# A transformer pair on one core: 96 bytes ahead of the weight tiles, the last strip's banks, the order of the constant tables, and one copy on another engine

## The chip, the cores and the metric

The kernel runs on one core of a Trainium2 chip. The metric is the device time of one execution in microseconds (us). Of the kernel before there are three timed executions, and one more that was profiled. Engines: TensorE (PE, with its weight loads PEld), VectorE (DVE), ScalarE (ACT), GpSimd (POOL), and SyncE (SP), which here only issues DMAs.

## The reference, cut to what matters

Two transformer blocks run one after the other over x, 256 tokens of 1024 channels in fp32. Each linear layer below is a product of the (normed) tokens with a weight matrix; together with the tables they make nearly all of the 191.47 MB read.

```python
# first block
h = rmsnorm(x, norm_mix)
fq, fk, fv, ff, gq, gk, gv, gb, ga, gz, sq, sk, sv, gates = split(h @ w_in)
ya = fox_attention(...); yb = gated_delta_rule(conv(gq, gk, gv), ...); yc = stick_breaking_attention(...)
x = x + (g0 * (ya @ w_oa) + g1 * (yb @ w_ob) + g2 * (yc @ w_oc)) @ w_out
x = x + memory_cross_attention(rmsnorm(x), rmsnorm(mem), w_mq, w_mkv, ..., w_mo)
x = x + conv_ffn(rmsnorm(x), w_up, ffn_conv, ffn_conv_b, w_down)
# second block
x = x + 0.5 * rmsnorm(swiglu(rmsnorm(x), ...), ffn1_post_g)
x = x + rmsnorm(concat(moba_attention(...), multiscale_pool(...)) @ w_out, mix_post_g)
x = x + rmsnorm(memory_cross_attention_2(...), xa_post_g)
x = x + 0.5 * rmsnorm(swiglu(rmsnorm(x), w_gate, w_up, w_down), ffn2_post_g)
```

`rmsnorm(x, g)` is x / sqrt(mean(x*x) + 1e-6) * g over the 1024 channels.

## The kernel before, in words

**Layout and pieces.** The tokens lie channel by channel (128 partitions, 8 groups, 256 tokens) in `x`. Every weight matrix is streamed from HBM once, in pieces of at most 128 x 1024 fp32 (512 KB). A piece lands in `raw` (three buffers, `load_weight`, issued on SP), is then split by `split_weight` into a high part `wh` (ACT copies it, rounded to the type fp32r that PE multiplies) and a low part `wl` (DVE, `raw` less `wh`), four buffers each. Activations are split in the same way into `hi` and `lo` tiles of the pool `a`. PE forms three products for each piece, hi·wh, lo·wh and hi·wl, and adds them up in banks of PSUM.

**Jobs and banks.** A job is a strip of output columns of one layer, with one to several pieces. Kind "a" has the weights stationary and 256 tokens moving (matmuls 128x256), kind "b" has the activation stationary and 512 weight columns moving (128x512). A job takes its banks from the pool `pmm` (three banks, `PMM`) when its first piece starts, in `products`, and gives them back when its callback has evicted them. All the small work beside it (attention, the delta rule, norms), called chains, works in the pool `pat` (five banks, `LIMIT`), which `room`, `take` and `drop` share out. The names in the profile follow: `pmm<-a,wh` is a product of a weight piece, `pat<-...` a chain's matmul, and `raw`, `wh`, `wl` are the piece's tiles.

**Who sets the order.** All instructions are put out in one order by a planner that runs while the program is built. `Pace` (`issue`) models each engine's time with costs written in the code; `Stream.pick` takes the next piece from a window of split pieces, by `start_of`, which returns None for a job that hasn't begun as long as the `pmm` banks in use and its own would be more than three. Between pieces, `step` advances the chains (generators that are due) and calls `split`, which splits a piece and asks for the loads up to three pieces on. On the chip each engine then works through its own queue in that order, with semaphores between engines; the DMAs of one queue are issued in the order in which SP meets them. The order of the first strips is `FIRST_ORDER`.

**The start (from line 2013).** SP issues `x` in four parts with the first weight pieces between them, then `vec` (line 2025: gains and convolution taps, all but the few columns that an earlier DMA on ACT's queue, `vec0`, brought). A chain `constants` asks for the first half of `con` once 5 pieces have been loaded, for its second half at 9 and for `poolw` at 40. `start` splits the activations, `start_sq` squares x and adds up the squares, and `sq_rows` turns the sum into a row `rb` of 1/sqrt for all tokens: it adds the two halves (`one`), splits the sum into `hi` (a copy on ACT) and `lo` (a subtraction on the engine it is given, DVE for the first norm, GpSimd for the others), sums over partitions with a matmul with ones into a `pat` bank, and takes Ln and Exp on ACT. The first jobs' evictions multiply by `rb`, so they can't run before it.

**The end.** `result` (line 1536) is the last layer, 2816 to 1024 channels, with two jobs of kind "b", one for each half of the output channels; each job has two banks, one for each 128 tokens. The second job is made with `last=True`; its `held` list keeps the last two pieces back, and `last_pieces` runs them first for the one bank and then for the other. The first job's callback `cb` squares and multiplies both banks on ACT and DVE.

**Pools.** The pools are allocated in SBUF in the order x, c, a, s2, s1, tiny, sq, rb, wh, wl, raw (`build`, line 2042).

## Time and profile before

| | |
|---|---|
| median of 3 runs | 1154.55 us (1153.91 to 1156.99) |
| profiled execution | 1154.29 us, span 1152.5 us, mean granted clock of PE 0.994 |
| PE | 98% of the span busy, 9108 matmuls |
| DVE, ACT, POOL | 66%, 58%, 22% |
| DMA | 193.96 MB in all, 168 GB/s over the span |

The span runs from the first to the last recorded instruction. A row of a timeline gives start, length, engine, line, operation, output<-inputs, size and count, and in brackets how long the engine had been idle and what released it; the line is nearly always L291, that of the helper through which the planner issues. [...]

### The profile page before, as it was taken

What the parts mean: (1) busy time and instruction counts of PE and PEld (TensorE: products, weight loads), DVE (VectorE), ACT (ScalarE), POOL (GpSimd) and SP (SyncE); (2) the same over time, 40 slices, a digit from 0 to 9 for tenths busy, and PEclk for the clock granted to TensorE, in tenths of its full rate; (3) what the DMA queues carried; (4) which work ended last, traced back from release to release, by engine and by line L of the source; (5) the groups of instructions that cost most, each with busy time, mean ns of one, the idle gap of its engine ahead of it and who ended that gap; (6) DMA issues with size and microseconds to landing.
All of it is one profiled execution on the core that took longest, in us unless ns stands there. A gap on an engine that the chain in (4) does not pass through costs nothing.

```text
span 1152.5 us, 22341 instructions
## 1 busy us (share of the span) xinstructions
PE 1126.1 (98%) x9108; PEld 1074.6 (93%) x9108; DVE 762.5 (66%) x1015; ACT 668.1 (58%) x1085; POOL 250.1 (22%) x235
## 2 busy tenths in 40 slices
PE   8999999999999999999999999999999998999997
PEld 7998998999988999999999999999989998999976
DVE  6885785558886588998556555448876747555543
ACT  5447773465786566666545554546667557555442
POOL 0020130022141023333015333012102112533200
PEclk9999999999999999999999999999999999999999
DMA  7554533236564365556656555665444534666652
GB/s 244 180 170 152 193 111 111 93 111 199 169 200 146 101 193 183 183 183 190 203 160 218 191 190 177 201 194 160 167 148 147 152 92 140 205 192 207 196 191 91
DMA packets 56550, 193.96 MB, mean 168 GB/s; under 512 B 6400, under 2 KB 6528, under 8 KB 56448
## 3 DMA queue, kind: packets, MB, share of 16 engines
q1 hardware_dynamic: 56304, 192.54, 52.3%
q8 instruction: 71, 1.16, 0.4%
q14 instruction: 31, 0.25, 0.1%
q10 hardware_dynamic: 144, 0.01, 0.0%
HBM read 191.47 MB, written 1.05 MB: 167 GB/s over the span
## 4 chain that ended last, share of the span: by engine, by line
PE 65%; DVE 16%; ACT 7%; issue 6%; DMA 4%; POOL 1%; SPq 0%; DVEq 0%; ACTq 0%; POOLq 0%
PE pmm L291 58%; PE pat L291 8%; DVE wl L291 6%; ACT wh L291 3%; DVE s L291 3%; DVE a L291 3%; DMA raw<-w_in 3%; ACT s L291 2%; DVE g L291 1%; DMA raw<-w_up 1%; DVE sg L291 1%; DVE ypad L291 1%; POOL s L291 1%; ACT g L291 1%; ACT L291 1%
## 5 line engine op out<-in xcount | busy, mean ns | idle before, releaser
L291 DVE TENSOR_TENSOR wl<-raw,wh 128x1024 fp32r<-128x1024 f32 (+1 forms) x370 | 455.3, 1238 | 283.1 <-ACT wh L291 279.4
L291 PE MATMUL pmm<-a,wh 128*128 128x256 f32 x3856 | 505.0, 281 | 7.2 <-DVE a L291 5.2
L291 PEld LDWEIGHTS pmm<-a,wh 128*128 128x128 f32 x3856 | 474.3, 189 | 13.3 <-DVE a L291 6.9
L291 ACT ACTIVATE wh<-raw 128x1024 fp32r<-128x1024 f32 (+1 forms) x370 | 372.5, 1019 | 166.4 <-PE pmm L291 58.1
L291 PE MATMUL pmm<-a,wl 128*128 128x256 f32 x1928 | 269.8, 281 | 2.4 <-DVE wl L291 1.8
L291 PEld LDWEIGHTS pmm<-a,wl 128*128 128x128 f32 x1928 | 244.0, 188 | 5.8 <-DVE wl L291 4.4
L291 PE MATMUL pmm<-g,wh 128*128 128x256 f32 x1088 | 140.3, 280 | 0.1
L291 PEld LDWEIGHTS pmm<-g,wh 128*128 128x128 f32 x1088 | 132.6, 188 | 0.8 <-POOL g L291 0.3
L291 POOL TENSOR_TENSOR sq<-sq,sq 128x512 f32<-128x512 f32 x30 | 41.9, 1398 | 342.4 <-ACT sq L291 304.9
L291 POOL TENSOR_TENSOR s<-s 128x256 f32<-128x256 f32 x66 | 71.9, 1089 | 175.7 <-ACT s L291 169.3
L291 ACT ACTIVATE s<-s 128x256 f32<-128x256 f32 (+4 forms) x118 | 56.1, 478 | 91.2 <-DVE s L291 76.9
L291 POOL TENSOR_TENSOR g<-s,g 128x256 fp32r<-128x256 f32 x66 | 64.5, 978 | 60.0 <-ACT g L291 60.0
L291 PE MATMUL pmm<-g,wl 128*128 128x256 f32 x544 | 75.6, 280 | 0.0
L291 PEld LDWEIGHTS pmm<-g,wl 128*128 128x128 f32 x544 | 68.7, 188 | 0.1
L291 ACT ACTIVATE g<-s 128x256 fp32r<-128x256 f32 x66 | 27.3, 413 | 56.7 <-POOL s L291 56.7
L291 PE MATMUL pmm<-wh,g 128*128 128x512 f32 x208 | 55.4, 405 | 2.9 <-DVE a L291 1.9
L291 POOL TENSOR_TENSOR s<-s,s 128x512 fp32r<-128x512 f32 (+1 forms) x25 | 33.4, 1342 | 105.7 <-ACT s L291 101.0
L291 PEld LDWEIGHTS pmm<-wh,g 128*128 128x128 f32 x208 | 39.8, 193 | 13.0 <-DVE a L291 2.2
L291 DVE SCALAR_TENSOR_TENSOR s<-ypad,vec,s 128x256 f32<-128x256 f32 x88 | 45.7, 578 | 0.0
L291 PE MATMUL pmm<-wh,a 128*128 128x512 f32 x160 | 42.0, 401 | 0.0
L291 DVE TENSOR_TENSOR s<-pmm,rb 128x512 f32<-128x512 f32 x44 | 30.2, 688 | 16.1 <-PE pmm L291 16.1
L291 ACT ACTIVATE a<-x,vec 128x256 fp32r<-128x256 f32 x54 | 24.8, 501 | 21.5 <-DVE x L291 21.4
(165 smaller groups left out, 874.5 us busy)
## 6 DMA issues: line engine op xcount, KB each, us to landing
raw<-ffn_w_up SPq DMA_DIRECT2D x82, 512.0 KB, 4.2
raw<-w_in SPq DMA_DIRECT2D x78, 512.0 KB, 4.3
raw<-ffn_w_down SPq DMA_DIRECT2D x42, 512.0 KB, 4.3
raw<-w_up SPq DMA_DIRECT2D x41, 512.0 KB, 4.3
raw<-w_down SPq DMA_DIRECT2D x20, 512.0 KB, 4.3
raw<-w_out SPq DMA_DIRECT2D x16, 512.0 KB, 4.4
raw<-xa_wkv SPq DMA_DIRECT2D x16, 512.0 KB, 4.0
raw<-w_mkv SPq DMA_DIRECT2D x8, 512.0 KB, 4.1
```

Source lines behind the costliest of these rows:

```text
L291: return fn(*args, **kwargs)
```

## The change: four edits

1. A pool `gap` with one tile of 24 fp32 (96 bytes in each partition) is allocated between `rb` and `wh`, so that `wh`, `wl` and `raw` lie 96 bytes higher.
2. The last job (the one with a `held` list) takes its two banks from `pat`. In `start_of`, such a job no longer counts as a user of `pmm`; it may start when two `pat` banks are free in the model.
3. The DMA of `vec` moves from right behind the x loads into the chain `constants`, where it is asked for once 6 pieces have been loaded; the first half of `con` moves from 5 to 9, the second from 9 to 26. `poolw` stays at 40.
4. In `sq_rows`, the copy to `hi` runs on DVE when the engine given is DVE, which is so for the first norm alone.

```diff
+GAP = 24
...
         if job not in self.begun:
-            live = sum(len(j.ps) for j in self.begun + self.pending)
-            if live + job.banks > PMM - (pc is not self.window[0]):
+            live = sum(len(j.ps) for j in self.begun + self.pending if j.held is None)
+            if job.held is not None:
+                if len(self.K.live["pat"]) < job.banks or sorted(self.K.live["pat"])[job.banks - 1] > self.pace.now + SLACK:
+                    return None
+            elif live + job.banks > PMM - (pc is not self.window[0]):
                 return None
...
         if job.ps is None:
-            job.ps = [K.pmm() for _ in range(job.banks)]
+            if job.held is None:
+                job.ps = [K.pmm() for _ in range(job.banks)]
+            else:
+                job.ps = [K.pat().rearrange("p (a b) -> p a b", a=2) for _ in range(job.banks)]
             self.begun.append(job)
...
         hi, lo = (parts2[:, i, :] for i in range(2))
-        nc.scalar.activation(hi, one, AF.Copy)
+        if eng is nc.vector:
+            nc.vector.tensor_copy(hi, one)
+        else:
+            nc.scalar.activation(hi, one, AF.Copy)
         self.tt(lo, one, hi.bitcast(F32), ALU.subtract, eng)
...
-    nc.sync.dma_start(K.vec, aps["vec"][:, NVEC0:])
 
     def constants():
         half = CON["negtri"][0]
-        for n, dst, src in ((5, K.con[:, 0:half], aps["con"][:, 0:half]), (9, K.con[:, half:], aps["con"][:, half:]),
-                            (40, K.poolw, aps["pool_w"])):
+        for n, dst, src in ((6, K.vec, aps["vec"][:, NVEC0:]), (9, K.con[:, 0:half], aps["con"][:, 0:half]),
+                            (26, K.con[:, half:], aps["con"][:, half:]), (40, K.poolw, aps["pool_w"])):
...
-        pools = {n: (pool(n, b, **({"space": PSUM} if n in ("pmm", "pat") else {})), b) for n, b in bufs.items()}
+        pools = {}
+        for n, b in bufs.items():
+            if n == "wh":
+                pools["gap"] = (pool("gap", 1), 1)
+            pools[n] = (pool(n, b, **({"space": PSUM} if n in ("pmm", "pat") else {})), b)
         K = Kern(tc, pools, aps)
+        K.p["gap"].tile([P, GAP], F32, name="gap")
```

## Rows read from the trace of the kernel before

**Rows 1.** The page, busy time of each engine.

```profile
PE 1126.1 (98%) x9108; PEld 1074.6 (93%) x9108; DVE 762.5 (66%) x1015; ACT 668.1 (58%) x1085; POOL 250.1 (22%) x235
```

**Rows 2.** Windows, `pmm` matmuls alone: window, its length, PE busy (count), clock, DMA share, GB/s.

```profile
0.00:1153.00 1153.00, 1032.02 (x7968) 0.99 0.53 168
```

**Rows 3.** Timeline of PE: three stretches of the same products.

```profile
1010.55 2.03 PE L291 MATMUL pmm<-a,wh 128*128 128x256 f32 x16
1012.42 1.09 PE L291 MATMUL pmm<-a,wl 128*128 128x256 f32 x8
...
300.98 2.04 PE L291 MATMUL pmm<-g,wh 128*128 128x256 f32 x16
302.87 1.10 PE L291 MATMUL pmm<-g,wl 128*128 128x256 f32 x8
...
598.98 2.08 PE L291 MATMUL pmm<-a,wh 128*128 128x256 f32 x16
600.90 1.12 PE L291 MATMUL pmm<-a,wl 128*128 128x256 f32 x8
```

**Rows 4.** Timeline of PE and of DVE near the start.

```profile
26.25 0.50 PE L291 MATMUL pat<-onesr,s 128*128 128x1 f32 x4
29.50 0.88 PE L291 MATMUL pmm<-a,wh 128*128 128x256 f32 x4 [2.75 <-DVE a L291]
...
25.55 0.42 DVE L291 TENSOR_TENSOR s<-s,s 128x256 fp32r<-128x256 f32 x1
...
27.55 1.23 DVE L291 TENSOR_TENSOR wl<-raw,wh 128x1024 fp32r<-128x1024 f32 x1 [0.23 <-ACT wh L291]
```

**Rows 5.** Timeline of PE near the end.

```profile
1114.16 0.39 PE L291 MATMUL pmm<-wh,g 128*128 128x512 f32 x1
1115.59 0.97 PE L291 MATMUL pmm<-wh,g 128*128 128x512 f32 x3 [1.04 <-DVE sg L291]
```

**Rows 6.** Timeline of SP's DMA issues near the start.

```profile
15.98 0.43 SPq L291 DMA_DIRECT2D con<-con  x1
...
22.19 0.33 SPq L291 DMA_DIRECT2D raw<-w_in  x1
```

**Rows 7.** Chain that ended last, near the start: start, length, what.

```profile
17.53 5.68 DMA raw<-w_in
```

**Rows 8.** DMA issues: count, KB each, median us from issue to landing.

```profile
raw<-w_in SPq DMA_DIRECT2D x78, 512.0 KB, 4.3
...
con<-con SPq DMA_DIRECT2D x1, 800.0 KB, 5.5
con<-con SPq DMA_DIRECT2D x1, 404.0 KB, 4.6
vec<-vec SPq DMA_DIRECT2D x1, 172.5 KB, 5.0
```

**Rows 9.** Timeline of ACT near the start.

```profile
23.32 1.06 ACT L291 ACTIVATE wh<-raw 128x1024 fp32r<-128x1024 f32 x1 [2.67 <-DMA raw<-w_in]
24.28 0.40 ACT L291 ACTIVATE s<-s 128x256 fp32r<-128x256 f32 x1
...
26.46 1.06 ACT L291 ACTIVATE wh<-raw 128x1024 fp32r<-128x1024 f32 x1 [0.40 <-PE pat L291]
27.43 0.46 ACT L291 ACTIVATE rb<-pat,vec 128x258 f32<-128x258 f32 x1
```

**Rows 10.** Windows: window, its length, busy PE, PEld, DVE, ACT, POOL, clock, DMA.

```profile
29.92:33.34 3.42, 3.42 (x18) 3.42 (x17) 3.35 (x9) 3.02 (x6) 0.00 (x0) 0.50 0.97 378
33.34:36.75 3.41, 3.41 (x31) 3.41 (x30) 3.34 (x7) 1.43 (x2) 0.00 (x0) 1.00 0.03 8
```

**Rows 11.** Timeline of ACT and DVE: the first readers of `vec` and `con`.

```profile
30.07 1.31 ACT L291 ACTIVATE g<-ypad,vec 128x256 f32<-128x256 f32 x3 [1.74 <-DVE ypad L291]
...
48.78 0.69 DVE L291 TENSOR_TENSOR_SCAN row<-con,row 68x256 f32<-68x256 f32 x1
...
122.80 0.42 DVE L291 TENSOR_TENSOR s<-s,con 128x256 f32<-128x256 f32 x1
```

## The prediction

> **What bounds the kernel now.** I read the page first, for the engine that has no room left, then TensorE's rows for what its time is made of, and then the places where it waits. TensorE (PE) is busy for 1126.1 of 1152.5 us, 98% [rows 1]. The products of the weight pieces with the activations, all the matmuls whose output is a `pmm` bank, are 7968 instructions, and together they cover 1032.0 us at a mean granted clock of 0.99 [rows 2]. The reader is to see two things in this. Whatever is done on VectorE (DVE), ScalarE (ACT) or a DMA queue counts only where TensorE stands still for it, and the idle sum is only 26.4 us. And a change that touches every one of the 7968 matmuls by one nanosecond is worth 8 us, as much as a third of all the idle time.

> So the cadence comes next. The same instruction, 128x256 in fp32r, is not always equally fast: sixteen of them from 1010.55 to 1012.42 are 1.87/16 = 116.9 ns apart, sixteen from 300.98 to 302.87 are 118.1 ns, sixteen from 598.98 to 600.90 are 120.0 ns, all at full clock [rows 3]. Nearly all of the run stands at the first value, in which case 1032 us is its floor.

> Then the two waits on the path that this change touches. Near the start, PE idles for 2.75 us until 29.50, for `a` from DVE [rows 4]: all three `pmm` banks are full, and their eviction wants the first norm's row `rb`. At the end, the last strip's second 512-column matmul starts 1.43 us after its first (1115.59 less 1114.16) and has waited for DVE's `sg`, an eviction of the job before [rows 5].

> The profiled execution took 1154.29 us with a span of 1152.5, so 1.8 us lie around the span; the median of the three runs is 1154.55. I sum against 1154.29 and add 0.2 at the end for that difference.

> **The change part by part.**

> *The last strip's banks.* The last job takes two banks of `pat`, whose chains are done by then, and no longer waits for the eviction of the strip before. What is left is the ordinary distance of two 512-column matmuls, twice 116.9 = 234 ns: 1.43 − 0.23 = **1.2 us saved**. Everything behind it moves up, since PE runs on from there without an idle gap and the last evictions follow its end. Below this, nothing is saved if something else is late at the same place; the piece is split and its activation is there, as its first matmul has run. The rule that lets the last job start outside the `pmm` count moves nothing else, since the job before it stands ahead in the window. I keep 0 and −1.3 as ends.

> *The constant tables.* On the SP queue, the first half of `con` (404 KB, 4.6 us from issue to landing) stands at 15.98 in front of the piece issued at 17.53, which takes 5.68 us to land where the median of such pieces is 4.3 [rows 6 to 8]. ACT has then been idle for 2.67 us and takes the piece at 23.32 [rows 9]. In its place the change puts `vec` (172.5 KB [rows 8]); `con`'s first half goes where the 800 KB of its second half [rows 8] stood (26 us), and the second half goes out behind piece 26, some 70 us in. The queue ahead of the piece at 17.53 becomes shorter by 404 − 172.5 = 231.5 KB. At 378 GB/s (the rate of the stretch from 29.92 [rows 10]), that is 0.6 us.

> How much of this reaches PE? Follow the norm back from 29.50 [rows 4, 9]. The evictions wait for `rb`, whose first half (Ln) runs on ACT at 27.43, straight behind the split copy `wh` at 26.46; that copy is the one of the piece issued at 22.19 (22.19 + 4.3 = 26.5 [rows 6, 8]), so the norm waits in ACT's queue behind a landing. On DVE the split `wl` at 27.55 stands ahead of the evictions in the same way. The issue at 22.19 does not move, as it waits for an earlier split to free its buffer; what moves is its landing, because the two pieces before it have drained earlier. I take **0.5 us saved**: less than the 0.6 that the queue gives, as a landing in 3.7 us or so is the quickest that I would expect of 512 KB. The floor behind it: the norm's matmuls in PE's own queue end at 26.25 + 0.50 = 26.75, and Ln can't start before that, so at most 27.43 − 26.75 = 0.68 is there to be had. Ends: 0 (the landing stays as it is) and −0.68. What is late next is `rb` itself and the eviction, which stay.

> The later uses: `vec` is first needed by the convolution's taps at 30.07, `con`'s first half by a scan at 48.78, its second half at 122.80 [rows 11]. `vec` issued near 16 lands near 21, the first half issued near 26 near 31, the second half issued near 70 near 76. All are in time by 9 us or more, so no wait is added. The 800 KB put near 70 delay one weight piece by 800/378 = 2.1 us at most, once; the same bytes leave the stretch around 30, where the DMA share is 0.97 [rows 10]. PE has three split pieces in hand (2.8 us each, three times 24 matmuls at 117 ns), so I cost it at **nothing**; without that cover it is +2.1, and if the earlier stretch had been limited by those bytes, −0.5.

> *The norm's high part on DVE.* ACT loses a copy of 0.40 us at 24.28 [rows 9], DVE gets one ahead of the subtraction at 25.55 [rows 4]. That subtraction reads two tiles of this size and takes 0.42 us on DVE; a copy reads one, so I put it at no more than 0.4. Behind it on DVE stand the subtraction, which PE's norm matmuls wait for, and the next splits. The piece ahead of it on DVE comes 0.6 us earlier, by the same shorter queue, and a hop from ACT back to DVE goes, so the subtraction is not later than before. **Nothing**; ends: −0.1 and, if it delays the split at 27.55, +0.4.

> *The gap.* It adds no instruction. The 96 bytes shift the addresses of `wh`, `wl` and `raw`, hence every operand that ACT, DVE, PE and the DMA queues read or write for the weights. What could that change? Nothing in the rows ties a duration to an address: the three values of [rows 3] belong to the same tiles and the same shapes, and I found the same pairs of buffers in all of them. From above the price is bounded by the whole run falling from 116.9 to 118.1 ns, 7968 × 1.2 = +9.6 us, or at 120.0 to +24.7; from below by the slower stretches going away, at a tenth of the matmuls (my estimate of their number) × 1.2 ns = −1.0. I take **0**, because most of the run already has the lower value and a shift of all three tiles by one amount leaves their places relative to each other as they are.

> [...]

> The sum: 1154.29 − 1.2 − 0.5 = 1152.6, and 0.2 for the median: **1152.8 us**, 0.15% faster.

> **The rivals.**

> *A, faster: the shorter wait at the start also keeps the clock up.* [...] If the wait became so short that the clock stayed, 13 × 0.117 = 1.5 us more would go: 1151.3. For it: the wait is the only thing ahead of the fall. Against it: by my sum 2.2 of 2.75 us stay. Chance 0.18.

> *B, slower: the addresses matter for PE after all.* If the shift puts the weight reads into the slower cadence of 118.1 for the whole run, the time is 1152.8 + 9.6 = 1162.4. It decides from the point where the other gains are eaten and 0.3% is passed: (3.5 + 1.7)/0.0012 = 4300 of 7968 matmuls. For it: three cadences exist and something selects them. Against it: nothing in the rows selects them by address. Chance 0.10.

> [...] Chance 0.03.

> *D, it does not do what it says: the bank of the last strip was not all that was late, or the earlier landing is swallowed by ACT's queue.* Then one or both terms are zero, up to 1154.5. Chance 0.08.

> The forecast itself has 0.61.

> **How the numbers follow.** A difference of 0.3% (3.46 us: under 1151.1 or over 1158.0) is about what a measurement here tells from no change. The forecast's own ends are 1152.8 − 0.1 − 0.2 − 0.5 − 0.1 − 1.0 = 1150.9, all lower ends together, and 1152.8 + 1.2 + 0.5 + 2.1 + 0.4 = 1157.0, all covers gone together. The range reaches down to A with the same lower ends, 1151.3 − 1.9 = 1149.4, and up to 1156.6, just inside the upper end; outside lie B, C and little else. Faster by over 0.3%: C, half of A (its value lies beside the limit), and 0.11 for the forecast with the gap's lower end, 0.23. Slower: B and 0.01 for a delay that I haven't seen, 0.11. Between them 0.66.

> **What would show it.** In the profile after: the last strip's second 512-column matmul about 0.23 us behind its first, with no idle time put down to DVE `sg`; `vec` issued near 16 and the following piece landing in under 5.2 us; PE's idle ahead of the first long run near 2.2 us, followed by 18 matmuls at half clock (A: 31); no wait for a DMA longer than before near 70 to 80 us; sixteen 128x256 matmuls at 1.87 us near 1010, and the whole `pmm` group at 1032 less the 1.2 or so. I am wrong if the `pmm` group's busy time moves by more than 3 us with the count the same: then addresses select the cadence. I am wrong in a term if the idle at the end or at the start is as long as before.

## The result, and the profile after

The changed kernel takes 1143.43 us (median of 4 runs, 1141.36 to 1145.09) against 1155.28 us before; the ratio is 0.9896, with a 95% interval of 0.9871 to 0.9920. I had forecast 1152.8 with a range from 1149.4 to 1156.6. The profiled execution took 1144.74 us, 9.55 less than the one of before.

Ahead of everything else, the page's first lines, which answer to [rows 1]:

```profile
span 1142.9 us, 22344 instructions
...
PE 1111.7 (97%) x9108; PEld 1060.7 (93%) x9108; DVE 761.7 (67%) x1016; ACT 667.8 (58%) x1084; POOL 251.6 (22%) x235
```

The reader is to take two differences from them. TensorE's busy time fell by 1126.1 − 1111.7 = 14.4 us with the same 9108 matmuls, and its idle time rose by 31.2 − 26.4 = 4.8 us; together these are the 9.6 us by which the span is shorter. So the matmuls themselves became cheaper. The timeline of PE in two stretches shows it (start, length, operation, count), and answers to [rows 3]:

```profile
621.27 1.98 PE L292 MATMUL pmm<-a,wh 128*128 128x256 f32 x16
623.08 1.07 PE L292 MATMUL pmm<-a,wl 128*128 128x256 f32 x8
...
1011.26 2.05 PE L292 MATMUL pmm<-a,wh 128*128 128x256 f32 x16
1013.14 1.11 PE L292 MATMUL pmm<-a,wl 128*128 128x256 f32 x8
```

From 621.27 to 623.08, start to start, there are 16 matmuls in 1.81 us, 113 ns each: a cadence that the kernel before never held for a stretch. (The row's own length, 1.98, reaches past the start of the next row.) From 1011.26 to 1013.14 the same instruction with the same address class takes 117.5. Averaged over long stretches the two are 113.33 and 117.78 ns. Over all 7170 or so distances between neighbouring 128x256 matmuls, the mean went from 116.87 to 114.89 ns (7416 x 1.98 = 14.7 us), and that of the 512-column matmuls from 233.2 to 229.6 (552 x 3.6 = 2.0 us). The two make 2.3 us more than the busy time shows; that difference is not resolved.

In this profile the start became worse, not better. Timelines of PE, of SP's issues and of ACT, then windows (window, length, busy PE, PEld, DVE, ACT, POOL, clock, DMA), which answer to [rows 4, 6, 9, 10]:

```profile
26.37 0.50 PE L292 MATMUL pat<-onesr,s 128*128 128x1 f32 x4
31.04 3.75 PE L292 MATMUL pmm<-a,wh 128*128 128x256 f32 x16 [4.16 <-DVE a L292]
...
16.38 0.42 SPq L292 DMA_DIRECT2D vec<-vec  x1
17.73 4.71 SPq L292 DMA_DIRECT2D raw<-w_in  x3
22.49 0.43 SPq L292 DMA_DIRECT2D con<-con  x1
...
27.91 1.06 ACT L292 ACTIVATE wh<-raw 128x1024 fp32r<-128x1024 f32 x1 [2.19 <-DMA raw<-w_in]
28.87 0.46 ACT L292 ACTIVATE rb<-pat,vec 128x258 f32<-128x258 f32 x1
...
30.19:33.60 3.41, 2.56 (x12) 2.59 (x13) 3.37 (x9) 2.08 (x5) 0.00 (x0) 0.50 0.57 201
33.60:37.02 3.42, 3.42 (x18) 3.42 (x18) 3.42 (x10) 1.64 (x2) 0.00 (x0) 0.50 0.04 14
```

PE idles for 4.16 us where it idled for 2.75, and the half clock behind it (granted 0.50) lasts for 6.8 us where it lasted for 3.4. The piece that the norm waits for was issued at 22.11 and landed at 27.81; `con`'s first half went out at 22.49, right behind it. One profile of each kernel is not enough to lay this on the edit: in a second profile of the changed kernel the idle is 3.08 us, and in one of a kernel with the gap and the banks alone, its tables where they were before, it is 4.08. Timelines of PE, in this order:

```profile
29.84 1.43 PE L292 MATMUL pmm<-a,wh 128*128 128x256 f32 x6 [3.08 <-DVE a L292]
```

```profile
30.14 1.22 PE L292 MATMUL pmm<-a,wh 128*128 128x256 f32 x4 [4.08 <-DVE a L292]
```

The end did what was forecast (timeline of PE, answers to [rows 5]): the last strip is now `pat<-wh,g`, follows without a break, and eight matmuls take 1.84 us, 230 ns each.

```profile
1106.50 2.00 PE L292 MATMUL pat<-wh,g 128*128 128x512 f32 x8
1108.34 1.07 PE L292 MATMUL pat<-wl,g 128*128 128x512 f32 x4
```

Where the other idle time comes from is in PE's waits (who waited for whom: total us, times, longest), the changed kernel's:

```profile
PE pmm L292 <- DVE a L292: 7.6, 7, 4.2
PE pmm L292 <- DVE wl L292: 3.2, 7, 1.1
PE pmm L292 <- ACT wh L292: 3.1, 6, 1.5
PE pat L292 <- POOL s L292: 2.9, 4, 1.4
```

In the kernel before these rows read 7.0, 1.8, 1.7 and 1.6. With cheaper matmuls PE reaches the splits and the chains before these are done: 1.4 + 1.4 + 1.3 us of the gain were given back there; with 1.4 more at the start and 1.0 less at the end this is nearly all of the 4.8. The next two runs bear it out: with the gap alone PE idles for 32.3 us, with the three other edits alone for 27.3.

### The profile page after: what moved, and what is told of

It is laid out like the page before. It is cut to its first block, busy times and chain, and to the rows that moved or that the text cites. A ratio compares the mean times of both kernels' runs of the same rounds, so it can differ in the third digit from the quotient of the medians.

```text
span 1142.9 us, 22344 instructions
## 1 busy us (share of the span) xinstructions
PE 1111.7 (97%) x9108; PEld 1060.7 (93%) x9108; DVE 761.7 (67%) x1016; ACT 667.8 (58%) x1084; POOL 251.6 (22%) x235
## 4 chain that ended last, share of the span: by engine, by line
PE 67%; DVE 14%; ACT 7%; issue 5%; DMA 4%; POOL 1%; DVEq 0%; ACTq 0%; POOLq 0%
PE pmm L292 56%; PE pat L292 11%; DVE wl L292 6%; ACT wh L292 3%; DVE a L292 2%; DVE s L292 2%; DVE g L292 2%; ACT s L292 1%; DMA raw<-w_in 1%; DVE sg L292 1%; ACT L292 1%; DMA raw<-ffn_w_up 1%; DVE ypad L292 1%; ACT g L292 1%; POOL s L292 1%
## 5 line engine op out<-in xcount | busy, mean ns | idle before, releaser
L292 PE MATMUL pmm<-a,wh 128*128 128x256 f32 x3856 | 498.1, 280 | 9.7 <-DVE a L292 5.8
L292 PEld LDWEIGHTS pmm<-a,wh 128*128 128x128 f32 x3856 | 468.1, 189 | 16.0 <-issue 5.1
L292 PE MATMUL pmm<-g,wh 128*128 128x256 f32 x1088 | 137.4, 278 | 0.4 <-DVE g L292 0.4
L292 PEld LDWEIGHTS pmm<-g,wh 128*128 128x128 f32 x1088 | 130.1, 188 | 1.0 <-DVE g L292 0.6
L292 ACT ACTIVATE g<-s 128x256 fp32r<-128x256 f32 x66 | 27.3, 413 | 56.8 <-POOL s L292 56.8
L292 PEld LDWEIGHTS pmm<-wh,a 128*128 128x128 f32 x160 | 29.4, 188 | 6.8 <-DVE g L292 0.7
L292 DVE SCALAR_TENSOR_TENSOR a<-x,vec,a 128x256 fp32r<-128x256 f32 x56 | 32.9, 622 | 2.3 <-ACT a L292 2.3
```

The costliest lines, as they stand in the source:

```text
L292: return fn(*args, **kwargs)
```

## The experiments

The theory after the result (G): the gap alone gives the gain, because the start addresses of weights and activations set the cadence. Rivals: O, the order of the constants or the engine of the copy gives it; and of the addresses, W (the weights' alone), R (weights and moving tile relative to each other), H (not they, but history and traffic).

**Each half of the change by itself.** The kernel before with only the gap, and the changed kernel without it:

```diff
# e1_gap_only: before, and
+GAP = 24
+                pools["gap"] = (pool("gap", 1), 1)
+        K.p["gap"].tile([P, GAP], F32, name="gap")
# e2_no_gap: after, without these three lines
```

> The kernel before with the gap of 96 bytes and no other edit. Theory G (the gap alone gives the gain, through TensorE's cadence): 1144 us (1142 to 1147), the 128x256 cadence 113.3 ns over long stretches as in the changed kernel, idle at the start 2.75 us and the 1.43 us at the end unchanged. Rival O (the order of constants, or the engine of the copy, gives it): 1155 us, cadence 116.9.

> The changed kernel without the gap, the three other edits kept. Theory G: 1154.5 to 1157 us (the 1.2 us of the last strip saved, some 2.5 to 3 us lost at the start, where TensorE's idle is 4.2 us and the half clock lasts 6.8 us), cadence 116.9. Rival O: 1143 to 1145 us.

The gap alone: 1141.27 us (1140.73 to 1145.20), ratio 0.9883 (0.9866 to 0.9900). Without it: 1155.9 us, ratio 1.0000 (0.9986 to 1.0014). G holds and O falls: the three other edits together are worth nothing that can be measured. The lines of busy time from the two pages, the gap alone first, then the change without it:

```profile
PE 1106.6 (97%) x9108; PEld 1054.9 (93%) x9108; DVE 761.8 (67%) x1015; ACT 669.1 (59%) x1085; POOL 251.8 (22%) x235
```

```profile
PE 1125.9 (98%) x9108; PEld 1075.8 (93%) x9108; DVE 763.0 (66%) x1016; ACT 668.5 (58%) x1084; POOL 253.1 (22%) x235
```

Only PE and PEld differ, by 19 and 21 us; DVE and ACT, which read and write the same shifted tiles, stay within 1.2 us.

**TensorE alone, 20 pairs of addresses.** 

```diff
+STA = (0, 4, 8, 16, 24)      # fp32 past a multiple of 128 bytes: weights
+MOV = (0, 8, 16, 24)         # moving tile
+for r in range(2):
+    for s in STA:
+        for m in MOV:
+            stop()           # a small matmul that waits for DVE
+            config(s, m, 8)  # 8 pieces of 24 matmuls 128x256
```

> This kernel computes none of the blocks: TensorE alone multiplies zeros, in the kernel's own pattern (pieces of 24 fp32r matmuls 128x256: hi.wh, hi.wl, lo.wh, a weight load each), with nothing else running. The weights start 0, 16, 32, 64 or 96 bytes past a multiple of 128 bytes, the moving tile 0, 32, 64 or 96 bytes past one, all 20 pairs, each for 192 matmuls, the whole list twice. Theory W (the weights' address alone sets the cadence): about 113.3 ns at one class of the weights' address (0 and 64, or 0 alone), 116.7 at 32 and 96, whatever the moving tile's. Theory R (the address of weights and moving tile relative to each other): the fast pairs form a diagonal of the table. Theory H (addresses are not it, only the history of the run and the other engines' traffic): one cadence for all 20 pairs, or another one in the second pass than in the first.

Mean ns from one matmul to the next at full clock, by the bytes past a multiple of 128 (where the second pass differs by over 0.5 it stands behind a stroke):

| weights \ moving | 0 | 32 | 64 | 96 |
|---|---|---|---|---|
| 0 | 120.0 / 118.7 | 117.8 / 116.7 | **113.3** | 120.0 |
| 16 | 118.3 | 120.0 | 116.7 | 117.8 |
| 32 | 120.0 | 120.0 | 117.3 | 117.8 |
| 64 | **113.3** | 120.0 | 120.0 | 118.7 |
| 96 | 116.7 / 117.8 | 117.8 | 120.0 | 120.0 |

Two rows of its timeline for each of two pairs, weights/moving 0/0 and 64/0; each row is a piece of 24, 2.88 and 2.72 us from start to start:

```profile
15.61 3.04 PE L1363 MATMUL pmmb<-moa,wha 128*128 128x256 f32 x24
18.49 3.04 PE L1363 MATMUL pmmc<-moa,wha 128*128 128x256 f32 x24
...
307.80 2.88 PE L1363 MATMUL pmmc<-moa,whd 128*128 128x256 f32 x24
310.52 2.88 PE L1363 MATMUL pmma<-moa,whd 128*128 128x256 f32 x24
```

Apart from the small writes between the pairs no other engine worked in this time, so H falls as the whole story: addresses count. W falls too, since 0 and 64 are each fast with one moving tile and slow with the other three. R holds in part. The fast pairs are no diagonal, as 32/96 and 96/32, which also lie 64 apart, take 117.8; the two fast ones are those with both tiles on multiples of 64 bytes, in opposite halves of 128. In the kernel, `a` starts at 44608 and `g` at 93760, both 64 past a multiple of 128, and all their buffers are 4096 bytes apart; `wh` starts at 184096 before (32 past: the pair 32/64) and at 184192 after (the pair 0/64). These addresses are those of the compiled programs. Three pairs had two cadences in two passes, so something besides the addresses counts too. And the table is not the kernel: the pair 32/64 takes 117.3 here, but 116.7 or 117.8 over long stretches of the kernel before. Why is not shown; the kernel takes the products in another order.

**The same in the kernel.** A gap of 32 bytes gives the pair 64/64; 64 bytes ahead of `a` and 96 ahead of `wh` give 64/0.

```diff
# g32_same_parity: e1_gap_only with
-GAP = 24
+GAP = 8
# s64_swapped: e1_gap_only with a second gap
+        K.p["gapa"].tile([P, 16], F32, name="gapa")   # ahead of the pool a
```

> The kernel before with a gap of 32 bytes in place of none (the changed kernel has 96) and no other edit: the weights then start 64 bytes past a multiple of 128, as the activations do. Theory R (fast only where weights and moving tile both lie on multiples of 64 bytes and in opposite halves of 128): the pair 64/64 ran at 120.0 ns alone, so the cadence is near 120 and the time 1155.5 + 8520 x 3.1 ns = about 1180 us (1172 to 1184). Theory W (weights on a multiple of 64 bytes are enough, the moving tile does not matter): 113.3 ns and 1141 us, as with 96 bytes.

> The kernel before with 64 bytes ahead of the pool of the activations and 96 ahead of the weights: activations on a multiple of 128 bytes, weights 64 past one, the changed kernel's pair the other way round. No other edit. Theory R: 113.3 ns in long stretches and 1139 to 1145 us, as with the gap alone. Rival (the weights must lie on multiples of 128, or it is the distance to raw or to the edge of the memory that counts): no gain, 1155 us or more.

32 bytes: 1166.97 us, ratio 1.0081 (1.0057 to 1.0106), slower than with no gap at all. The direction is R's and against W; the size that I had put on it (1172 to 1184 us) was some 2.5 times too large. The 128x256 cadence rose by 3.0 ns as expected (119.88 in the mean), but a 512-column matmul fell from 233.2 to 228.0, and part of the rest had been idle time of PE before (26.4 us, here 1165.1 − 1142.2 = 22.9). Swapped: 1151.1 us (1143.38 to 1157.08), ratio 0.9943 (0.9916 to 0.9969): a gain, so not the distance to `raw` or to the memory's edge; but smaller and much more scattered than forecast. The profiled one (1145.33, among the fastest of the eight) has 113.3 over the same stretch in which 32 bytes have 120; what the slower ones, up to 1157.08, held was not profiled. Timelines of PE, 32 bytes first, then swapped:

```profile
1011.21 2.08 PE L292 MATMUL pmm<-a,wh 128*128 128x256 f32 x16
1013.13 1.12 PE L292 MATMUL pmm<-a,wl 128*128 128x256 f32 x8
```

```profile
1010.29 1.98 PE L292 MATMUL pmm<-a,wh 128*128 128x256 f32 x16
1012.11 1.07 PE L292 MATMUL pmm<-a,wl 128*128 128x256 f32 x8
```

**What holds a stretch at 117.8 with the good addresses.** TensorE alone again, with interruptions between blocks of 48 matmuls:

```diff
+for (s, m) in ((0, 16), (16, 0), (8, 16)):   # in fp32
+    for kind in range(5):                    # five interruptions
+        for r in range(10):
+            stop(kind); two pieces of 24 matmuls
# m3_kicks: two pairs, nine kinds of odd matmul in place of the waits
```

> This kernel computes none of the blocks: TensorE alone multiplies zeros in the kernel's pattern, 48 matmuls at a time, and between these one of five interruptions, ten times each: a small matmul waiting for DVE, a wait for the weights, a wait for the moving tile, two plain fp32 matmuls 128x256, four plain fp32 matmuls 128x1. Three pairs of addresses past a multiple of 128 bytes (weights/moving): 0/64, 64/0, 32/64 (the kernel before). Theory P (each interruption leaves the two streams in another phase, and the phase stays until the next one): in 0/64 and 64/0 some stretches run at 113.3 ns and others at 117.8, each uniform, the mixture depending on the kind of interruption; 32/64 at 116.7, 117.8 or 120. Rival T (117.8 in the changed kernel comes from the traffic of the other engines): all stretches of the first two pairs at 113.3 after every kind of interruption.

> This kernel computes none of the blocks: TensorE alone multiplies zeros in the kernel's pattern, 48 matmuls at a time, with one of nine things between them, eight times each: nothing; one matmul of 16, 32 or 128 columns; one whose moving tile lies 64 bytes higher; one whose weights lie 64 bytes higher; one of 240 columns; a small matmul that waits for DVE; three plain fp32 matmuls of one column. Pairs 0/64 and 64/0 in turn. Theory P (two states of the same addresses, told apart by the phase of weight reads and moving reads, in which the stream stays until something shifts it): with nothing in between one cadence throughout, 113.3 or 117.8; some of the odd matmuls switch it, always the same way for the same state. Rival (each restart is a new draw): no pattern over the eight repetitions, the mixture the same after any of them.

In the first, the waits for weights and moving tile told nothing, as DVE's write had been done before PE got there. The pair 0/64 ran at 113.3 behind the small matmul and behind plain 128x256 fp32 matmuls; behind four plain matmuls of one column it alternated strictly, 117.8, 113.3, five times over. The pair 64/0 stood at 117.8 throughout, behind the four plain matmuls too, ten times of ten. The pair 32/64 had 117.3 and 118.7 behind the small matmul and the four plain ones, and 120.0 in nine of ten blocks behind the plain 128x256 ones; I had expected 116.7, 117.8 or 120. T falls as the whole story, as 117.8 comes behind the plain matmuls with no other engine at work.

In the second, 0/64 began at 117.8 and stayed there for 64 blocks, whatever stood between them, until three plain fp32 matmuls of one column put it at 113.3, where it stayed behind all eight. 64/0 switched in periods of four or two blocks behind some of the odd matmuls, stood at 117.8 behind the one whose moving tile lies higher and at 113.3 behind the one whose weights do, and at 113.3 behind the three plain ones, eight of eight. Of these 16 kicks, as I call the three plain ones, only the first found 117.8 ahead of it. So in these two runs the same addresses had two cadences, 113.3 and 117.8 ns, a stretch kept the one that it had, and the next one went by what came between, in a fixed pattern where nothing waited. Behind the small matmul that waits for DVE, 64/0 had 113.3 three times, 117.8 four times, then 113.3 again; eight blocks don't tell whether a wait is a draw. What it is that lasts was not measured; "phase" is only my name for it.

Timelines of the two runs follow; a plain fp32 matmul shows as two rows there, so three of them as x6 and four as x8. First 64/0 in the first run, 2.83 us (117.9 a matmul) from 555.52 to 558.35 ahead of four plain matmuls:

```profile
555.52 2.99 PE L1360 MATMUL pmmb<-mob,whb 128*128 128x256 f32 x24
558.35 0.95 PE L1360 MATMUL pz<-zf 128*128 128x1 f32 x8
559.15 3.07 PE L1360 MATMUL pmmc<-mob,whb 128*128 128x256 f32 x24
562.06 2.99 PE L1360 MATMUL pmma<-mob,whb 128*128 128x256 f32 x24
564.89 0.95 PE L1360 MATMUL pz<-zf 128*128 128x1 f32 x8
```

Then 0/64 in the second run around the first kick: 377.58 to 380.40 is 24 matmuls in 2.82 us (117.5), 383.80 to 386.52 is 2.72 (113.3):

```profile
377.58 2.99 PE L1360 MATMUL pmma<-moa,wha 128*128 128x256 f32 x24
380.40 0.72 PE L1360 MATMUL pz<-zf 128*128 128x1 f32 x6
380.99 2.97 PE L1360 MATMUL pmma<-moa,wha 128*128 128x256 f32 x24
383.80 2.88 PE L1360 MATMUL pmmb<-moa,wha 128*128 128x256 f32 x24
386.52 0.72 PE L1360 MATMUL pz<-zf 128*128 128x1 f32 x6
```

**The kick in the kernel.**

```diff
+            if pc["src"][:2] in KICKS and K.live["pat"] and min(K.live["pat"]) <= self.pace.now:
+                kick = K.pat()
+                for _ in range(3):
+                    K.mm(kick[:, 0:1], K.ones(), K.ones()[:, 0:1], True, True)
+                K.drop(pat=1)
# b2_kicked: KICKS = (("ffn1_w_up_2", 2), ("ffn2_w_up_2", 2)); b3: strip 6 of each in place of 2
```

> The gap and the last strip's banks (as in the kernel of b1_gap_and_banks), and three plain fp32 matmuls of one column ahead of the third strip of each of the second block's two up-projections, where the longest uninterrupted stretches of 128x256 matmuls begin; alone, these left the stream at 113.3 ns 16 times of 16, from either state. Theory P: both long stretches (near 600 to 770 and 965 to 1085 us) run at 113.3 ns; the median is that of b1 or up to 5 us below it (two kicks cost 2 x 0.6 us, a stretch at 117.8 costs 6.5 or 4 us), and the runs spread less than b1's. If in the kernel the state is set by other things as well: one of the stretches at 117.8, time and spread as b1's.

> As b2_kicked, with the three plain fp32 matmuls moved from the third to the seventh strip of each up-projection, so that they stand inside the two long stretches and not ahead of the last wait before them. Theory P: behind the kick both stretches run at 113.3 ns whatever they ran at before it (b2's second kick stood at 952 us, ahead of a wait near 970, and the stretch behind that wait was at 117.8); median 1140 to 1143 us, spread under 5 us. If the kick only toggles the state, or does nothing in the kernel: one of the stretches at 117.8 behind it in some profile, median 1144 to 1148.

> The same kernel as b3_kick_inside, one more profile. Theory P: 113.3 ns behind both kicks again. Toggling or no effect: 117.8 behind a kick in about one stretch of three.

> The same kernel as b3_kick_inside, a third profile. Theory P: 113.3 ns behind both kicks again. Toggling or no effect: 117.8 behind a kick in about one stretch of three.

The first was put in a bad place: its second kick stood at 952 us, PE waited near 970, and the stretch behind that wait ran at 117.78; the median is 1147.96 us (1144.15 to 1157.22). With the kicks inside the stretches, all six (three profiles) have 113.33 behind them. Five had it ahead of the kick as well; the sixth is the one that tells a reset. Timeline of PE in the second profile, 117.5 ahead of 990.77 and 113.8 behind 994.17 (117.78 and 113.33 over longer stretches):

```profile
987.94 2.05 PE L293 MATMUL pmm<-a,wh 128*128 128x256 f32 x16
989.82 1.10 PE L293 MATMUL pmm<-a,wl 128*128 128x256 f32 x8
990.77 0.72 PE L293 MATMUL pat<-onesr 128*128 128x1 f32 x6
...
994.17 1.98 PE L293 MATMUL pmm<-a,wh 128*128 128x256 f32 x16
995.99 0.28 PE L293 MATMUL pmm<-a,wl 128*128 128x256 f32 x1
```

A toggle is excluded by the other five. That a kick resets the slower cadence rests on two cases, this one and the first in TensorE alone; the other 20 found 113.3 and kept it, so that my "from either state" said more than I had. The time did not follow: 1144.04 us (1140.46 to 1146.43), and 1146.91 and 1143.30 in the two further profiled runs, where I had expected 1140 to 1143 with a spread under 5. A kick costs 0.6 us, and the two stretches were at 113.3 without it in most profiles.

**The edits at the start and the end.** The changed kernel with the tables asked for at other places, and with all but the gap and the banks undone:

```diff
# e3_later_con: vec behind the x loads as before, con's first half at 13
-        for n, dst, src in ((6, K.vec, ...), (9, K.con[:, 0:half], ...),
+        for n, dst, src in ((13, K.con[:, 0:half], ...),
# b1_gap_and_banks: constants and the copy of hi as before
```

> The changed kernel with vec asked for where it was before (behind the x loads) and the first half of con at 13 pieces instead of 9, so that no table stands between the pieces that the first norm's row waits for. If the first half of con beside piece 10 is what makes the start later (piece 10 lands at 27.8 instead of 26.4), PE's idle falls from 4.2 to 2.3 us or less, the half clock from 6.8 to 3.4, and the time is 2.5 to 4 us under the changed kernel's: 1139 to 1141 us. If the copy on DVE or something else is what is late: the idle stays near 4 us and the time near 1143 us.

> The changed kernel with the constants and the copy of the norm's high part as they were before: only the gap and the last strip's banks are left of the change. By the traces the gap alone is 1141.3 us, the banks take 1.2 to 1.4 us from the end, and the changed kernel loses 1.4 to 3 us at the start to the first half of con beside piece 10: 1139 to 1141 us, below both kernels. If the constants are not what costs at the start, 1143 us as the changed kernel.

> The same kernel as b1_gap_and_banks, on the chip of the other two. If its 1148.6 us there came from long stretches that fell into the slower of the two states and not from the kernel, another profile has other stretches in that state, and the times lie anywhere between 1139 and 1150 us. If it was the kernel: 1148 us again, with the stretch from 600 to 770 at 117.8 ns again.

> The changed kernel once more, beside the two others. Theory P: other stretches at 117.8 ns than in its first profile (there 965 to 1085 us), PE's idle at the start again about 4 us with the first half of con beside piece 10, 1141 to 1149 us. If the state of a stretch belongs to the kernel's own order: the same stretches as in its first profile.

With `con` later, PE came back at 29.61 in place of 31.04, after 3.52 us of idle where I had expected 2.3 or less, and the half clock lasted for 3.4 us again; the time is 1144.08 (1143.67 to 1146.76), so my 1139 to 1141 was a miss. This profile has falls of the clock at 112.7 and 949.0 that the changed kernel's first one lacks. Nor does the return of PE tell much: in the ten profiles of kernels with the tables where they were before, it lies anywhere between 28.72 and 30.76, and the half clock lasts for 3.4 or 6.8 us. The gap with the banks took 1148.57 us on one chip and 1143.82 on the next, where I had expected 1139 to 1141; the changed kernel took 1144.82 on the second. The profiles of the same kernel differ in which stretch has which cadence: 620 to 760 us at 117.78, then at 113.33, in the gap with the banks; 1000 to 1075 at 117.78, then at 113.33, in the changed kernel. The old pair 32/64 has two levels as well: the stretch behind 602 us ran at 116.67 in the kernel before and at 117.78 in the change without the gap. The 1487 matmuls of the first stretch times 4.45 ns are 6.6 us, most of what lies between the two profiled runs (1150.36 and 1142.31). Timelines of the gap with the banks, first and second profile:

```profile
650.34 2.05 PE L292 MATMUL pmm<-a,wh 128*128 128x256 f32 x16
652.23 1.10 PE L292 MATMUL pmm<-a,wl 128*128 128x256 f32 x8
```

```profile
649.94 1.98 PE L292 MATMUL pmm<-a,wh 128*128 128x256 f32 x16
651.75 1.07 PE L292 MATMUL pmm<-a,wl 128*128 128x256 f32 x8
```

No kernel here is shown to beat the gap alone (1141.27), and its interval overlaps that of the changed kernel.

## Why the prediction was wrong, point by point

**The gap: the step that failed.** I took 0, with the reason that nothing ties a duration to an address, as the same pairs of buffers have all three cadences. The observation was right and the inference wrong: every buffer lies a multiple of 4096 bytes from the next, so all pairs of [rows 3] are one and the same pair of classes, 32/64. A trace in which the address class never varies can't say what it does; it can say only that, within one class, something else varies too, and that is so (what I call the phase). My lower end, −1.0 us, let only the slower stretches go away, but the lowest value in a trace is not the lowest there is: 116.67 ns over long stretches before, 113.33 after. Measured: about 60% of the 128x256 matmuls at 113.3 and 30% at 117.8 in the changed kernel's first profile, 14.4 us less busy time; with the gap alone 19.5 us less, and 1141.27 us, 1.2% less, where I had put no gain at all. Two smaller slips: "nearly all of the run" at the first value was some 80%, and 552 of the 7968 matmuls that I multiplied by one cadence have 512 columns.

**Rival B** had the mechanism. That addresses matter was right, with the wrong sign for 96 bytes and with its sign for 32 (9.4 us more where it said 9.6, but that closeness is luck: the cadence rose by 3.0 ns and not by 1.2, and the 512-column matmuls and the idle time gave some of it back). **Rival C** stands in the chances with 0.03, for a time far below the forecast; no run shows the floor of a matmul that its size was worked out from. What the runs show is 113.3 ns as the lowest cadence that 128x256 matmuls held, against 116.67 before, and 1141.27 us as the lowest median. TensorE alone, with no other engine at work but for the small writes between the pairs, took 113.3 to 120.0 ns for the same matmul, by the addresses of the two tiles that it read and by what lasts.

**The last strip's banks: right** in the trace, 1.43 us became 0.23. No run shows these 1.2 us in the time.

**The constant tables: the 0.5 us did not come, and a loss is not shown.** The chain was read rightly: in all 14 profiles of whole kernels PE comes back 3.1 to 3.3 us after the landing of the piece issued near 22. The piece behind `vec` landed after 5.27 us in place of 5.68, where I had wanted under 5.2. The 3.7 us that I took for a quick landing of 512 KB was an estimate; in the kernel before, the 512 KB pieces have medians from 3.5 us (`w_mo`) to 4.4 us (`w_out`), for matrices of four pieces or more. What I had wrong is the place of the other table: `con`'s first half does not stand where the second half stood. That was behind the next piece, at 26.04; here it is asked for one piece earlier, at 22.49, since the planner's steps fell differently, and I had not followed its order. From issue to landing that piece took 5.69, 5.59 and 4.49 us in the three profiles with `con` right behind it, and 3.67 to 4.80 in the eleven others. Two of the three are longer than all the others, which speaks for `con`; but PE came back at 31.04, 30.70 and 29.84 in the three and between 28.72 and 30.76 in the eleven, so that what it costs in time stays open.

The 800 KB that went out at 70.66 cost nothing that shows: between 60 and 100 us PE idled for 0.36 us. There the cover held.

**The copy on DVE: as forecast**, 0.29 us, hidden. **Rival A**, worked out from the 31 − 18 matmuls of [rows 10] at granted clocks of 1.00 and 0.50, did not come: the idle grew. My sum left PE's other waits, for the splits and the chains, as they were; these gave back some 4 us once PE was faster.

## What to carry to other kernels

When one operation with one shape shows several cadences in a trace, its floor isn't known: measure it by itself over the start addresses of both operands before an edit of the layout is costed at nothing. Where weights stream against a moving tile as here (fp32r, 256 columns, a weight load each), try both on multiples of 64 bytes in opposite halves of 128: of the 20 pairs measured only those two reached 113.3 ns, and the gap that brought the kernel to one of them took it from 1156.38 to 1141.27 us. Expect some stretches at 117.8 even so (30% of these matmuls in the changed kernel's first profile), and check the addresses in the compiled program, as any tile allocated ahead moves them. And when a transfer is moved in an order that a planner writes, read the new order out; the old place is not kept.
